# A hybrid RWKV-7 / gated DeltaNet block: block inversions split in two, scores in natural layout, keys normed through token scalars

## The chip, the cores and the metric

The kernel runs on one core of one Trainium2 chip. The metric is the device time of one execution in microseconds (us); a time is the median of several runs. The engines of the core are TensorE (PE, matrix products into PSUM; its weight loads are counted apart as PEld), VectorE (DVE), ScalarE (ACT), GpSimd (POOL) and SyncE (SP, which here only issues transfers). Each engine runs its own instructions in order and waits for the others by semaphores.

## The reference

One layer over 256 latent tokens of width 2048 and a prefix of 256 context tokens. Both are normed and modulated, go through one input projection and through two token mixers, each in both directions: RWKV-7 with 16 heads of 64, and gated DeltaNet with 8 heads of 128. The mixers are merged through sigmoid gates; a SwiGLU feed-forward of hidden width 5632 and a last norm follow. The two recurrences are what the change is about:

```python
def rwkv7_scan(r, w, k, v, kk, bb, s0):
    def step(s, inp):
        r_t, w_t, k_t, v_t, kk_t, b_t = inp
        sa = jnp.einsum('bhij,bhj->bhi', s, kk_t)
        s = s * w_t[:, :, None, :] - sa[..., None] * b_t[:, :, None, :] + v_t[..., None] * k_t[:, :, None, :]
        return s, jnp.einsum('bhij,bhj->bhi', s, r_t)
...
def gdn_chunked(q, k, v, g, beta, s0):     # k and q come in l2-normed
...
    decay = jnp.where(incl, jnp.exp(jnp.where(incl, diff, 0.0)), 0.0)
    kb = kc * bc[..., None]
    lmat = jnp.where(strict, jnp.einsum('nbhik,nbhjk->nbhij', kb, kc) * decay, 0.0)
    rhs = jnp.concatenate([vc * bc[..., None], kb * jnp.exp(gc)[..., None]], axis=-1)
    sol = lax.linalg.triangular_solve(lmat, rhs, left_side=True, lower=True, unit_diagonal=True)
    u, wk = sol[..., :dv], sol[..., dv:]
...
    def step(s, inp):
        qk_i, u_i, w_i, qd_i, kt_i, gl_i = inp
        v_new = u_i - jnp.einsum('bhck,bhkv->bhcv', w_i, s)
        o = jnp.einsum('bhck,bhkv->bhcv', qd_i, s) + jnp.einsum('bhcj,bhjv->bhcv', qk_i, v_new)
        s = s * gl_i[..., None, None] + jnp.einsum('bhck,bhcv->bhkv', kt_i, v_new)
        return s, o
```

## The kernel before

**Stages.** A first stage (to 139 us) computes the modulation and the normed input and splits it into a high and a low fp32r part. The woven stage follows: all other input projections, both mixers and part of the modulation. Then come the merge products (`pa`, `pb`), the output projection, the feed-forward and the last norm, which the change leaves as they are. A full-precision product is made of three fp32r matmuls (weights high by input high, high by low, low by high), so each weight tile passes through a cast on ACT (`whi`) and a subtraction on DVE (`wlo`). These are the `mm` products; all other matmuls of the mixers are plain f32.

**The woven stage** is ordered by a planner, `Weave`, when the program is built. Every piece of work is a Python generator that yields the instructions it wants next, or the name of an event that it needs. A greedy loop keeps a modelled time for each engine and always issues the piece that can start first, with `RANK` to break ties; `LAT` holds the model's delays. The resulting order on PE, DVE, ACT and POOL is fixed in the program. `Words` and `Weave.late` model when PE's instructions arrive, in blocks of 256. The 40 gate products have no early consumer; `GATES_A` and `GATES_B` say after which pair or head each may be taken, and so they fill gaps.

**RWKV pairs.** Two heads of 64 make a pair, in the two halves of the 128 partitions; eight pairs run through `prepare` (decays, keys), `grams` (score matrices by 64-token chunks), `inverse`, `values` and `scan`. In `grams` the scores `X` and the decayed queries `laR` are stored with the heads' halves interleaved, so that masking and scaling take one instruction for each half. `inverse` inverts 16 unit-triangular 64x64 matrices a head through `invert`: the 16x16 diagonal blocks are transposed, sent to a scratch in DRAM (`scr`), read back as one block a partition, solved there by 15 steps of two small DVE instructions, sent back (`tscr`), and combined by small products on PE (`pi` banks) into 32 and 64. Pair p may not begin before the inversion of p - 1 has ended (`yield "inverse", p - 1`).

**DeltaNet heads.** Eight heads run through `features` (convolution, silu, norms by `l2n`), `tokens` (keys and values turned to token layout, keys scaled to `keg` and `kta`), `decays`, `head_grams`, `head_inverse` (the same `invert`, with eight 64x64 matrices, so that the substitution fills 64 partitions, and a last step to 128) and `head_scan`. The last computes `NW`, minus the solved keys, ahead of the recurrence; a step is then PE (solved values plus `NW` by state), DVE (`Vn`), PE (`kta` by `Vn`), DVE (`St`).

All of these go through `Lane.op` (line 148) and, on PE, `Words` (line 198), so they share these two lines in the profile and are told apart by their tiles; `arena` is one large tile in which many others lie, and `inX` another.

Of the kernel before, what the change touches and what calls it, by code (L numbers as in the profile page):

```python
# [11 lines left out]
F32 = mybir.dt.float32  # L12
# [6 lines left out]
P = 128  # L19
D = 2048  # L20
KT = D // P
T = 256
# [5 lines left out]
GATES_A, GATES_B = (6, 3, 2, 3, 0, 1, 4, 3), (3, 2, 0, 1, 1, 1, 9, 1)  # L28

RANK = dict(cast=-98, lowrank=164, prepare=59, grams=34, inverse=-70, values=-6, scan=-95, begin=196, head_scan=145, head_inverse=100, head_grams=132, decays=132, tokens=73, features=120, gate_out=137, lowrank_out=105, row_tile=496)  # L30
LAT = dict(dma=2.04, hop=0.2729, own=0.092, grp=32, cg=4, turn=0.17)
# [7 lines left out]
for _name, _w in (("ident", 128), ("ones", 128), ("bd64", 128), ("rmask", 256),  # L39
                  ("low16", 2), ("eye16", 32), ("tri", 256), ("aft", 256), ("past", 256), ("q4", 4), ("q2", 2),  # L40
                  ("eps", 1), ("gneps", 1)):
    _C[_name] = (_n, _n + _w)
    _n += _w
# [12 lines left out]
def const_array():  # L56
# [20 lines left out]
    put("past", np.where(np.concatenate([u <= v, u >= v], 1), 0.0, -200.0))  # L77
# [25 lines left out]
BLOCK = dict(size=256, first=193, ahead=40, time=4.2, base=8, waits=1.0072)  # L103
# [82 lines left out]
class Words:  # L186


    def __init__(self, engine):
        self.engine, self.n = engine, BLOCK["base"]  # L190

    def __getattr__(self, name):
        if name not in ("matmul", "transpose"):
            return getattr(self.engine, name)

        def op(out, a, *r, **k):
            self.n += (2 if name == "transpose" or a.dtype == F32R else 4) * BLOCK["waits"]
            return getattr(self.engine, name)(out, a, *r, **k)  # L198
        return op


class Weave:
# [5 lines left out]
    def __init__(self):  # L208
        self.work, self.free, self.done, self.now, self.kind = [], {}, {}, 0.0, "split"
        self.block, self.here, self.asked = None, 0.0, None  # L210
# [4 lines left out]
    def late(self, ops, start):  # L215

        n, t, b, here, asked, late = self.tensor.engine.n, start, self.block, self.here, self.asked, 0.0
        if b is None:
            b = int(n - BLOCK["first"]) // BLOCK["size"] + 1
        for o in ops:  # L220
            edge = BLOCK["first"] + BLOCK["size"] * b
            if asked is None and n >= edge - BLOCK["ahead"]:
                asked = max(t, here)
            if n >= edge:
                if t < here:
                    late += here - t
                    t = here
                b, here, asked = b + 1, (t if asked is None else asked) + BLOCK["time"], None
            n += self.words(o) * BLOCK["waits"]
            t += o.cost  # L230
        return late, (b, here, asked)
# [48 lines left out]
    def run(self):  # L280
        while self.work:
# [29 lines left out]
            if lane is self.tensor:  # L311
# [4 lines left out]
                self.block, self.here, self.asked = self.late(ops, start)[1]  # L316
# [9 lines left out]
def emit(ctx: ExitStack, tc, A, out, dbg=None):  # L326
    nc = tc.nc
    V, S, G, Q = nc.vector, nc.scalar, nc.gpsimd, nc.sync
    E = Words(nc.tensor)
# [35 lines left out]
    past = c_("past").rearrange("p (d t) -> p d t", d=2)  # L365
# [252 lines left out]
    def invert(pool, Lt, parts, nu, which, full, fill):  # L618
# [3 lines left out]

        h2 = nu // 2
        late = 0.0 if nu == 16 else 1.2
        sl, tl = scr[which], tscr[which]

        T0 = pool.tile([P, nu, 64], F32, tag="iv0", name="T0")
        Tx = pool.tile([P, nu, 64], F32, tag="ivx", name="Tx", bufs=2)  # L630
        us = (slice(0, h2), slice(h2, nu))
        flip = T0[:, us[0]]
        for h in range(2):
            r = slice(64 * h, 64 * h + 64)
            for u0, ap in parts(h, 0):
                yield v.transpose(flip[r, u0:u0 + ap.shape[1], :], ap)
# [1222 lines left out]
```

## Time and profile before

| | us |
|---|---|
| median of 3 runs | 2201.65 (2200.84 to 2202.81) |
| the profiled execution | 2203.45 |
| its span, first to last instruction | 2201.7 |
| first stage | 0 to 139 |
| woven stage | 139 to about 1238, its tail beside the first merge products to about 1300 |
| merge, output projection, feed-forward, last norm | to 2201.7 |

In the profile, a group of instructions is told as line, engine, operation, tiles written and read (out<-in), shape and count; then busy time in us, the mean of one in ns, and the idle time of the engine before them with what ended it. The kind MATMUL on PE appears twice for a plain f32 product. For a tile, the columns are shortest, median and longest duration in ns and the first and last start in us.

### The profile page before, as it was taken

What the parts mean: (1) busy time and instruction counts of PE and PEld (TensorE: products, weight loads), DVE (VectorE), ACT (ScalarE), POOL (GpSimd) and SP (SyncE); (2) the same over time, 40 slices, a digit from 0 to 9 for tenths busy, and PEclk for the clock granted to TensorE, in tenths of its full rate; (3) what the DMA queues carried; (4) which work ended last, traced back from release to release, by engine and by line L of the source; (5) the groups of instructions that cost most, each with busy time, mean ns of one, the idle gap of its engine ahead of it and who ended that gap; (6) DMA issues with size and microseconds to landing.
All of it is one profiled execution on the core that took longest, in us unless ns stands there. A gap on an engine that the chain in (4) does not pass through costs nothing.

```text
span 2201.7 us, 56730 instructions
## 1 busy us (share of the span) xinstructions
PE 2107.9 (96%) x23996; PEld 1906.1 (87%) x23996; DVE 1576.0 (72%) x3197; ACT 1068.0 (49%) x1852; POOL 121.7 (6%) x203
## 2 busy tenths in 40 slices
PE   6999899999999999999999899999999999999998
PEld 4766687878888778888889899999999999999997
DVE  3456788888898768999998789955665665544544
ACT  3249744554456345555545465534444444444443
POOL 0000000110000010111110010100000000000000
PEclk9999999999999999999999999999999999999999
DMA  9966543444444435666657878927777776566665
GB/s 386 413 178 197 153 127 104 120 123 114 120 120 130 115 105 183 194 184 193 185 186 257 292 282 306 347 85 233 236 232 233 236 236 201 189 186 188 191 186 161
DMA packets 234494, 435.29 MB, mean 198 GB/s; under 512 B 115328, under 2 KB 129664, under 8 KB 229888
## 3 DMA queue, kind: packets, MB, share of 16 engines
q1 hardware_dynamic: 206304, 355.11, 51.4%
q0 software_dynamic: 14112, 51.39, 7.0%
q10 hardware_dynamic: 13824, 25.17, 3.5%
q8 instruction: 188, 3.08, 0.6%
q14 instruction: 66, 0.54, 0.1%
HBM read 405.76 MB, written 25.84 MB: 196 GB/s over the span
## 4 chain that ended last, share of the span: by engine, by line
issue 41%; PE 11%; DVE 6%; DMA 3%; ACT 1%; POOL 1%; SPq 0%; POOLq 0%; DVEq 0%; ACTq 0%
PE mm L198 8%; DVE arena L148 2%; DMA aw<-ada_rest 2%; PE s L198 1%; DVE wlo L148 1%; DVE aw L148 1%; PE pa L198 1%; DMA wraw<-pa 1%; DVE inX L148 1%; PE pi L198 0%; DMA arena<-grow 0%; DVE wlo L413 0%; DMA inX<-tscr 0%; DVE LT L148 0%; ACT arena L148 0%
## 5 line engine op out<-in xcount | busy, mean ns | idle before, releaser
L413 DVE TENSOR_TENSOR wlo<-wraw,whi 128x1024 fp32r<-128x1024 f32 x328 | 392.4, 1198 | 320.6 <-ACT whi L412 318.4
L412 ACT CAST whi<-wraw 128x1024 fp32r<-128x1024 f32 x328 | 337.2, 1029 | 467.3 <-PE mm L198 417.5
L198 PE MATMUL mm<-hxh,wlo 128*128 128x256 f32 (+1 forms) x1408 | 474.8, 337 | 10.0 <-DVE wlo L148 9.3
L198 PE MATMUL mm<-hxh,whi 128*128 128x256 f32 (+1 forms) x1408 | 476.0, 338 | 5.7 <-ACT whi L148 3.2
L198 PE MATMUL mm<-hxl,whi 128*128 128x256 f32 (+1 forms) x1408 | 472.0, 335 | 0.0
L198 PE MATMUL mm<-hfh,wlo 128*128 128x256 f32 x1344 | 375.5, 279 | 0.4 <-DVE wlo L413 0.4
L198 PE MATMUL mm<-hfh,whi 128*128 128x256 f32 x1344 | 375.2, 279 | 0.0
L198 PE MATMUL mm<-hfl,whi 128*128 128x256 f32 x1344 | 375.2, 279 | 0.0
L198 PEld LDWEIGHTS mm<-hxh,wlo 128*128 128x128 f32 x1408 | 267.3, 190 | 39.1 <-DVE wlo L148 14.3
L198 PEld LDWEIGHTS mm<-hxh,whi 128*128 128x128 f32 x1408 | 267.4, 190 | 32.3 <-issue 6.8
L198 PEld LDWEIGHTS mm<-hxl,whi 128*128 128x128 f32 x1408 | 267.6, 190 | 24.6 <-issue 4.4
L148 ACT CAST whi<-wraw 128x512 fp32r<-128x512 f32 x344 | 204.6, 616 | 123.3 <-PE mm L198 82.3
L148 DVE TENSOR_TENSOR wlo<-wraw,whi 128x512 fp32r<-128x512 f32 x344 | 241.8, 704 | 27.8 <-ACT whi L148 24.9
L198 PEld LDWEIGHTS mm<-hfh,wlo 128*128 128x128 f32 x1344 | 252.6, 188 | 0.7 <-DVE wlo L413 0.6
L198 PEld LDWEIGHTS mm<-hfl,whi 128*128 128x128 f32 x1344 | 252.6, 188 | 0.0
L198 PEld LDWEIGHTS mm<-hfh,whi 128*128 128x128 f32 x1344 | 252.6, 188 | 0.0
L198 PE MATMUL mm<-za,whi 128*128 128x256 f32 x1024 | 180.2, 279 | 0.0
L198 PEld LDWEIGHTS mm<-za,whi 128*128 128x128 f32 x1024 | 156.1, 188 | 0.1
L148 DVE TENSOR_TENSOR arena<-arena 128x28 f32<-128x28 f32 (+13 forms) x538 | 138.9, 260 | 19.3 <-DMA arena<-scr 8.5
L198 PE MATMUL mm<-za,wlo 128*128 128x256 f32 x512 | 142.9, 279 | 0.0
L148 ACT ACTIVATE arena<-arena 128x512 f32<-128x512 f32 (+3 forms) x132 | 76.3, 592 | 72.1 <-DVE arena L148 49.2
L198 PEld LDWEIGHTS mm<-za,wlo 128*128 128x128 f32 x512 | 96.2, 188 | 0.0
(316 smaller groups left out, 3618.7 us busy)
## 6 DMA issues: line engine op xcount, KB each, us to landing
wraw<-w SPq DMA_DIRECT2D x172, 512.0 KB, 4.0
wraw<-wgu SPq DMA_DIRECT2D x168, 512.0 KB, 4.7
aw<-ada_rest POOLq DMA_DIRECT2D x96, 512.0 KB, 5.5
aw<-ada_first SPq DMA_DIRECT2D x32, 1024.0 KB, 14.1
wraw<-wdn SPq DMA_DIRECT2D x64, 448.0 KB, 3.6
wraw<-wout SPq DMA_DIRECT2D x32, 512.0 KB, 6.3
aw<-ada_gt ACTq DMA_DIRECT2D x64, 256.0 KB, 5.0
wraw<-wdn SPq DMA_DIRECT2D x32, 512.0 KB, 3.6
```

Of the source, the lines that this page charges most:

```text
L148: return Op(self, cost, lambda: getattr(self.engine, name)(out, *a, **k), kind)
L198: return getattr(self.engine, name)(out, a, *r, **k)
L412: S.copy(hi[:, c, :M], raw[:, c, :M])
L413: V.tensor_sub(lo[:, c, :M], raw[:, c, :M], hi[:, c, :M].bitcast(F32))
```

## The change

For the RWKV pairs, `invert` is split. `solve` does the transposes, the scratch transfers and the 16x16 substitution, in buffers of its own; `invert` does the rest. A pair's `solve` waits for the previous pair's `solve` and for the inversion before that; its `invert` still waits for the previous `invert`. Scores keep the natural layout: `X` has its masked scores in one slot for both halves, the queries are `rin`, their second scores `p2m`, and each is masked or scaled by one instruction over 128 partitions. The products that read them are 64x64 with both halves placed by hand, and the readout of `scan` makes two banks that are added. The identity in `KBx` is filled by ACT instead of POOL.

For the heads, `head_solve` makes the substitution for two heads at once on 128 partitions. Keys stay unnormed: `tokens` sums their squares a token on ACT, and the inverse norms go into the token scalars `gam`, which multiply the scores, the solved values and the values. `keg`, `kta` and `NW` are gone; from the second step on the recurrence computes key by state, corrects the values with it on DVE, then solves, scales on ACT (`Vs`, `Vn`) and updates the state. The decays are relu and exp on ACT instead of a subtraction on POOL and a minimum on DVE, with a mask for the first half alone. The score products with the queries move from `head_grams` to a piece of their own, `outputs`. Several buffers are deeper (keys 4, values, `LT` and outputs 3). `RANK`, `LAT['dma']`, `GATES_A`, `GATES_B` are other numbers, and PE's instruction supply is modelled as a rate with a cap instead of blocks.

```diff
-GATES_A, GATES_B = (6, 3, 2, 3, 0, 1, 4, 3), (3, 2, 0, 1, 1, 1, 9, 1)
+GATES_A, GATES_B = (5, 3, 2, 1, 0, 1, 5, 3), (3, 1, 0, 0, 2, 2, 9, 3)
...
-BLOCK = dict(size=256, first=193, ahead=40, time=4.2, base=8, waits=1.0072)
+BLOCK = dict(cap=160, rate=61.0)
...
+    def solve(pool, X, tt, flips, which, late, fill):
...
+        n = len(flips)
+        for i, (flip, part) in enumerate(flips):
+            u0, m = 16 // n * i, 8 // n
+            for h in range(2):
+                r = slice(64 * h, 64 * h + 64)
+                yield v.transpose(flip[r], part(h, 0))
+                w = dq(unit_rows(sl, h, u0, m), flip[r], 2)
+                w = dq(unit_rows(sl, h, u0 + m, m), part(h, 1), 2)
         yield w + late
...
+            yield v.tensor_mul(pr, X[:, j + 1:, j:j + 1].to_broadcast([P, n, m]), TT[:, j:j + 1, :m].to_broadcast([P, n, m]))
+            yield v.tensor_add(TT[:, j + 1:, :m], TT[:, j + 1:, :m], pr)
...
# prepare, grams
-            for j, h in enumerate(half):
-                yield v.tensor_mul(la[h, d, :, j, :], c3(r)[h], inc[h, 0:4, :])
+            yield v.tensor_mul(rin[:, d], c3(r), inc[:, 0:4, :])
...
-        for j in range(2):
-            h = half[1 - j]
-            yield v.tensor_mul(X[h, d, :, 1 - j, :], c3(p2[h]), mask(1 - d, 0, 8)(h))
+        yield v.tensor_mul(X[:, d, :, 0, :], c3(p2), mask(1 - d, 0, 8)(full))
...
+                yield s.copy(KBx[h, :, :, j, :].rearrange("p d c o -> p (d c) o"), ident[h, h].unsqueeze(1).to_broadcast([64, 16, 64]))
...
-        for j in range(2):
-            h = half[1 - j]
-            yield v.tensor_mul(la[h, d, :, j, :], c3(p2[h, 0:T]), mask(d, 64, 4)(h))
+        yield v.tensor_mul(p2m[:, d], c3(p2[:, 0:T]), mask(d, 64, 4)(full))
...
# inverse
         if p:
+            yield "halved", p - 1
+        if p > 1:
+            yield "inverse", p - 2
...
+        yield from solve(rs, end[:, 0:T], end[:, T:], [(Tx[:, 0:8], lambda h, d: LT[64 * h:64 * h + 64, d])], p % 2, 0.0, g)
+        weave.ready("halved", p)
+        if p:
             yield "inverse", p - 1
...
# features, tokens
-        yield from l2n(k, 512)
+        weave.ready("silu", h)
         yield from l2n(q, T, float(P) ** -0.5)
...
+        for b in range(4):
+            yield s.activation(kt[:, b], ps[:, P * b:P * b + P], AF.Square, accum_out=ssq[:, 0, h, b:b + 1])
+        yield s.copy(kt.rearrange("p b c -> p (b c)"), ps)
+        weave.release(pab)
+        yield s.activation(ssq[:, 0, h], ssq[:, 0, h], AF.Ln, bias=eps)
+        yield s.activation(ssq[:, 2, h], ssq[:, 0, h], AF.Exp, scale=-1.0)
+        yield s.activation(ssq[:, 1, h], ssq[:, 0, h], AF.Exp, scale=0.5)
+        for i, t in enumerate((nbtok, btok)):
+            yield v.tensor_mul(gam[:, i, h], t[:, :, h:h + 9:8], ssq[:, 2, h].unsqueeze(2).to_broadcast([P, 4, 2]))
+        weave.ready("norm", h)
+        yield v.tensor_mul(gam[:, 2, h], gam[:, 1, h], eta[:, :, h:h + 9:8])
...
+        for b in range(4):
+            yield s.activation(vt[:, b], ps[:, P * b:P * b + P], AF.Identity, scale=ssq[:, 1, h, b:b + 1])
-        for d in range(2):
-            col = 8 * d + h
-            late, soon = (slice(0, 4 - d), slice(d, 4))
-            yield v.tensor_mul(keg[:, d, late], p4[:, late], egc[:, late, col:col + 1].to_broadcast([P, 4 - d, P]))
-            yield v.tensor_mul(kta[:, d, soon], p4[:, soon], eta[:, soon, col:col + 1].to_broadcast([P, 4 - d, P]))
...
# decays
-            yield g.tensor_sub(ed, row, gct[:, :, col:col + 1].to_broadcast([P, 4, P]))
-            yield v.tensor_tensor(ed, ed, past[:, d].unsqueeze(1).to_broadcast([P, 4, P]), ALU.min)
-            yield s.activation(ed.rearrange("p b c -> p (b c)"), ed.rearrange("p b c -> p (b c)"), AF.Exp)
+            for b in range(4):
+                yield s.activation(ed[:, b], row[:, b], AF.Relu, bias=gct[:, b, col:col + 1], scale=-1.0)
+            yield s.activation(ed.rearrange("p b c -> p (b c)"), ed.rearrange("p b c -> p (b c)"), AF.Exp, scale=-1.0)
+            yield v.tensor_mul(ed[:, 0:2], ed[:, 0:2], tri[:, d].unsqueeze(1).to_broadcast([P, 2, P]))
...
# head_scan
-        NW = gs.tile([P, 2, 3, P], F32, tag="NW", name="NW")
-        for d in range(2):
-            ps = yield psb
-            yield [e.matmul(ps[:, P * i:P * i + P], keg[:, d, b, :], tf[:, 4 * d + b, :], start=True, stop=True)
-                   for i, b in enumerate(gorder[d][1:])]
...
+            if n:
+                ps = yield psb
+                yield [e.matmul(ps[:, P * d:P * d + P], k[:, P * bs[d]:P * bs[d] + P], St[:, d, :], start=True, stop=True) for d in range(2)]
+                r2 = gs.tile([P, 2, P], F32, tag="rt", name="rt")
+                for d in range(2):
+                    yield v.scalar_tensor_tensor(r2[:, d, :], ps[:, P * d:P * d + P], egc[:, bs[d], 8 * d + h:8 * d + h + 1],
+                                                 rt[d], ALU.mult, ALU.add)
...
-            for d in range(2):
-                yield v.tensor_scalar_mul(Vn[:, d, :], ps[:, P * d:P * d + P], btok[:, bs[d], 8 * d + h:8 * d + h + 1])
+            Vs, Vn = (gs.tile([P, 2, P], F32, tag="Vn", name="Vn") if use else None for use in (n < 3, n > 1))
+            for i, t in ((2, Vs), (1, Vn)):
+                for d in range(2 if t is not None else 0):
+                    yield s.activation(t[:, d, :], ps[:, P * d:P * d + P], AF.Identity, scale=gam[:, i, h, bs[d], d:d + 1])
```

More of the change, by code (lines that the diff above doesn't have):

```diff
@@ L215, in late @@
     def late(self, ops, start):
-        n, t, b, here, asked, late = self.tensor.engine.n, start, self.block, self.here, self.asked, 0.0
-        if b is None:
-            b = int(n - BLOCK["first"]) // BLOCK["size"] + 1
+        left, t, late = self.left + (start - self.seen) * BLOCK["rate"], start, 0.0
         for o in ops:
[L221 to L229, printed above, removed]
+            left, w = min(left, BLOCK["cap"]), self.words(o)
+            if left < w:
+                late += (w - left) / BLOCK["rate"]
+                t += (w - left) / BLOCK["rate"]
+                left = w
+            left += o.cost * BLOCK["rate"] - w
             t += o.cost
-        return late, (b, here, asked)
+        return late, left, t
     def add(self, rank, gen, at=None):
@@ L315, in run @@
                 self.kind = ops[-1].kind
-                self.block, self.here, self.asked = self.late(ops, start)[1]
+                _, self.left, self.seen = self.late(ops, start)
             w[5] = rest or None
@@ L994, in inverse @@
             if d < 2:
-                yield quad([e.matmul(ps[j][r, 64 * c:64 * c + 64], X[half[1 - j], d, c, a], KB[half[1 - j], d, c, :],
-                                     start=True, stop=True) for c in range(8) for j in range(2) for a, r in enumerate(half)])
+                yield quad([e.matmul(ps[j][half[1 - j ^ a], 64 * c:64 * c + 64], X[half[1 - j], d, c, a], KB[half[1 - j], d, c, :],
+                                     start=True, stop=True) for c in range(8) for j in range(2) for a in range(2)])
                 for j in range(2):
@@ L1390, in head_grams @@
         yield "decay", h
+        yield "norm", h
+        yield "mats", NPAIR - 1 if h else NPAIR - 2
+        if h > 1:
+            yield "inverse", NPAIR - 1
+        if h > 2:
+            yield "inv", h - 3
+        k, Ed = o["k"], o["Ed"]
+        o["LT"] = LT = gs.tile([P, 8, P], F32, tag="LTh" if h % 3 == 2 else "LTg", name="LT")
+        ps = yield pab
+        yield [e.matmul(ps[:, P * b:P * b + P], k[:, P * b:P * b + P], k[:, P * b:P * b + P], start=True, stop=True) for b in range(4)]
@@ L1565, in merge_rows @@
     def merge_rows():
-        for n in ("gram", "tok", "decay"):
+        for n in ("outs", "tok"):
             yield n, NGH - 1
```

336 lines of the change are left out of this document (172 added, 164 removed).

## The prediction

> **What bounds the kernel now.** I read the page's busy times first, then a table of stretches, then TensorE's waits, then the inversions' first and last starts, then single instructions for prices.
>
> ```profile
> PE 2107.9 (96%) x23996; PEld 1906.1 (87%) x23996; DVE 1576.0 (72%) x3197; ACT 1068.0 (49%) x1852; POOL 121.7 (6%) x203
> 139.00:1238.00 1099.00, 1048.87 (x14550) 880.77 (x14550) 929.49 (x2238) 591.82 (x1218) 99.84 (x161) 0.99 0.53 156
> 200.00:800.00 600.00, 566.49 (x9544) 469.75 (x9543) 494.54 (x1130) 326.04 (x699) 45.38 (x79) 0.98 0.45 123
> 800.00:1238.00 438.00, 424.15 (x4627) 369.41 (x4625) 398.33 (x1040) 219.70 (x438) 53.08 (x80) 0.99 0.63 194
> 1238.00:1300.00 62.00, 56.38 (x486) 54.19 (x487) 39.52 (x67) 36.26 (x55) 4.47 (x8) 0.92 0.82 295
> 1500.00:1600.00 100.00, 100.00 (x857) 99.87 (x856) 59.98 (x91) 42.98 (x54) 0.00 (x0) 1.00 0.73 234
> ```
>
> The columns of a stretch are its length, then busy PE, weight loads, DVE, ACT, POOL, the granted clock, DMA share and GB/s. The change touches only the woven stage, 139 to about 1300 us: RWKV pairs to 800, heads after. The feed-forward stretch (the last row) has PE at 100% and is not edited, so whatever is won before it is won at the end. In the woven stage PE idles 1099 - 1048.9 = 50.1 us, and 62 - 56.4 = 5.6 us in its tail: 55.7 us together. The gates' products fill its gaps. So the stage is as long as PE's work plus that idle time, and the time falls by PE work removed and idle time removed, nothing else. DVE comes next: 91% (398 of 438 us) in the heads.
>
> ```profile
> PE mm L198 <- DVE wlo L148: 9.3, 11, 3.1
> PE pi L198 <- DVE arena L148: 6.5, 8, 1.6
> PE s L198 <- DVE VX L148: 6.5, 11, 2.3
> PE mm L198 <- ACT whi L148: 3.2, 1, 3.2
> PE s L198 <- ACT arena L148: 2.6, 1, 2.6
> ...
> PE s L198 <- DVE Vn L148: 2.4, 5, 1.0
> PE pi L198 <- DMA arena<-tscr: 2.4, 1, 2.4
> ```
>
> These are PE's waits between 139 and 1300 us: total, times, longest. The `pi` rows, 6.5 + 2.4 = 8.9 us, are the inversions. Of the others DVE releases 9.3 + 6.5 + 2.4 = 18.2 us, ACT 5.8.
>
> ```profile
> L148 ACT COPY Pm<-pi x16: 577/580/585, 276.0 to 785.5; 64x512 f32<-64x512 f32 x16
> L148 DVE STREAM_TRANSPOSE inX<-LT x16: 422/432/444, 810.8 to 1197.3; 64x256 f32<-64x256 f32 x16
> L148 ACT COPY TF<-inX x16: 616/619/624, 861.1 to 1246.2; 64x512 f32<-64x512 f32 x16
> ```
>
> Two such instructions belong to each pair or head, so a period is a seventh of the distance: (785.5 - 276.0) / 7 = 73 us for a pair, (1246.2 - 861.1) / 7 = 55 us for a head. A head's inversion runs from its first transpose (810.8) to the copy into TF (861.1): 50 of the 55 us. The next may not start before, so the inversions set the pace, and the gates only hide it from PE.
>
> **The change, part by part. PE work.**
>
> ```profile
> 874.73 0.38 PE L198 MATMUL s<-inX,TF 128*128 128x128 f32 x2
> 874.94 0.39 PE L198 MATMUL s<-St,arena 128*128 128x128 f32 x2
> 875.17 0.39 PE L198 MATMUL s<-inX,TF 128*128 128x128 f32 x2
> ...
> 888.20 1.02 PE L198 MATMUL pa<-arena,C 128*128 128x512 f32 x2
> ...
> 889.29 0.40 PE L198 MATMUL mm<-hxl,whi 128*128 128x512 f32 x1
> 889.53 0.40 PE L198 MATMUL mm<-hxh,wlo 128*128 128x512 f32 x1
> L198 PE MATMUL s<-TF,keg 128*128 128x128 f32 x96 | 13.8, 283 | 0.0
> ```
>
> A plain f32 matmul leaves two records. From start to start a 128x128 one takes (875.17 - 874.73) / 2 = 0.22 us. The 512-wide one of the key norm takes 889.29 - 888.20 less the product slot behind it (889.53 - 889.29 = 0.24), 0.85 us. The change drops the products keg x tf, 96 records or 48 matmuls: 48 x 0.22 = 10.6 us. The keys are no longer normed across partitions, so eight 512-wide ones go: 8 x 0.85 = 6.8 us. NW x St becomes k x St and kta x Vn becomes kt x Vs, one for one; transposes and score products keep their number. **PE loses 17.4 us.** The natural score layout turns the readout's 16 matmuls of a pair into 32 of 64x64:
>
> ```profile
> L198 PE MATMUL s<-laR,VX 128*64 128x64 f32 x256 | 10.2, 226 | 1.2 <-DVE VX L148 1.0
> L198 PE MATMUL pa<-Pm,X 64*64 64x64 f32 x512 | 9.3, 221 | 0.0
> ```
>
> 256 records of the one took 10.2 us, 512 of the other 9.3: no change.
>
> **DVE and ACT work**, which counts only through PE's idle time:
>
> ```profile
> L148 DVE TENSOR_TENSOR X<-pa,C 64x512 f32<-64x512 f32 x32 | 22.0, 688 | 0.8
> L148 DVE TENSOR_TENSOR laR<-pa,C 64x256 f32<-64x256 f32 x32 | 13.5, 422 | 0.8
> L148 DVE TENSOR_TENSOR laR<-arena 64x256 f32<-64x256 f32 x32 | 13.3, 416 | 0.3
> L148 DVE TENSOR_TENSOR keg<-pa,egc x16: 517/615/691, 791.3 to 1171.4; 128x512 f32<-128x512 f32 x8, 128x384 f32<-128x384 f32 x8
> L148 DVE TENSOR_TENSOR kta<-pa,eta x16: 518/614/690, 792.6 to 1172.5; 128x512 f32<-128x512 f32 x8, 128x384 f32<-128x384 f32 x8
> L148 DVE TENSOR_TENSOR arena<-arena 64x63 f32<-64x63 f32 x32 | 6.9, 215 | 0.8
> L148 DVE TENSOR_TENSOR arena<-arena 64x15 f32<-64x15 f32 x32 | 5.3, 165 | 2.3 <-DMA arena<-scr 1.9
> L148 DVE TENSOR_SCALAR Vn<-s,btok 128x128 f32<-128x128 f32 x64 | 20.8, 338 | 4.7 <-PE s L198 4.6
> L148 DVE SCALAR_TENSOR_TENSOR St<-St,egl,s 128x128 f32<-128x128 f32 x32 | 10.4, 335 | 1.2 <-PE s L198 1.2
> L148 DVE SCALAR_TENSOR_TENSOR arena<-arena 128x512 f32<-128x512 f32 x24 | 19.6, 817 | 0.4 <-ACT arena L148 0.4
> L148 ACT COPY arena<-s 128x128 f32<-128x128 f32 x16 | 3.7, 270 | 10.6 <-PE s L198 10.6
> L148 ACT ACTIVATE arena<-arena 128x128 f32<-128x128 f32 x3 | 0.9, 311 | 0.0
> L148 ACT CAST whi<-wraw 128x512 fp32r<-128x512 f32 x344 | 204.6, 616 | 123.3 <-PE mm L198 82.3
> ```
>
> The first three rows are half-height pairs of instructions that become one full-height instruction of the same length: (22.0 + 13.5 + 13.3) / 2 = 24.4 us less. keg and kta go: 32 x 0.615 = 19.7. The substitution is 30 instructions a head at 165 to 215 ns, about 46 us in all; two heads at a time halve it, 23 less. Vn moves to ACT, 20.8. The key norm's last DVE pass, 8 x 0.817 = 6.5. The decay's masking shrinks to half its width, 16 x (0.688 - 0.422) = 4. New on DVE are the three corrections of each recurrence in both directions, 48 x 0.335 = 16.1, and 24 small factors at some 0.2, 5. **DVE loses 78 us.** ACT gains eighty scalings at 0.27 to 0.31 (23), sixty-four Relu passes at 0.311 (20), thirty-two squares (10), the identity fill moved from POOL, 16 of 64x1024 at some 1.0, an estimate from the 512-wide cast (16), 32 scaled copies of v at 0.27 in place of eight 512-wide, a key copy of 8 x 0.62 and small norms (13); it loses NW and three passes of each key norm, 16 x 0.5 + 24 x 0.62 (23). **ACT gains 59 us.** No DMA is added: scratch and substitution transfers of the heads fall from 10 a head to 9.
>
> The Trainium skill speaks against this exchange: "ScalarE: Activation LUTs", section "Rules for kernel authors", sends multiplications and relu to VectorE. The rows above disagree for this size, 270 ns on ACT against 338 on DVE, both from PSUM. By the page's own figure for a pointer operand (280 ns + 0.833 ns an element), an estimate of 387 ns each, the eighty scalings would be 31 us on ACT instead of 23, and the sum would stay.
>
> **PE's idle time** is the unknown term. Ends: all 55.7 us gone, or a chain that waits longer and brings back what the work saved (+17). Nearest rows: DVE's load over 139 to 1238 falls from 929/1099 = 0.85 to about 851/1071 = 0.79. If a wait grows as load/(1 - load), the 18.2 us behind DVE shrink by a third, 6 us; ACT's load rises from 0.54 to 0.61 and its 5.8 us grow by 2. The inversions stop setting the pace: a pair's substitution starts before the previous inversion ends, and half of the heads' go away. What is late next is PE itself, and the recurrences behind it. I credit this with 9 us, the `pi` rows whole. **Idle time: -6 + 2 - 9 = -13**, a quarter of the way to its lower end. The reorder of priorities and the new model of PE's instruction supply move work about, not its amount; I cost them at nothing, their cover being the gates' products, 40 before and after, and their price inside the two ends.
>
> Sum: -17.4 - 13 = -30.4 us against the profiled execution's 2203.45 (span 2201.7 and 1.75 around it), 2173. The median of the runs, 2201.65, lies 1.8 below that execution: **2171 us**.
>
> **Rivals.** *A, the forecast*: 2160 to 2184, chance 0.52.
>
> *B, the inversions were the true limit*: with the pace gone, most of the idle time goes (45 of 55.7) and the clock of 0.92 in the tail and 0.98 in the pairs rises, some 0.01 of 1161 us, 12 us: 2201.65 - 17.4 - 45 - 12 = about 2127, and up to 2155 if half of it comes true. For it: 50 of 55 us. Against: PE is 95% busy with the fillers, so shorter chains have little left to uncover. The Trainium skill's "Perfetto Trace Analysis", section "Identifying the Most-Contended Engine", judges TensorE by weight loads, not by matmul busy time; by that rule the woven stage (881 of 1099) is 80% used against 100% in the last stretch, which speaks for B. Chance 0.22.
>
> *C, the longer recurrence*: each step but the first now has PE, DVE, PE, ACT where it had PE, DVE.
>
> ```profile
> 1268.11 0.61 DVE L148 TENSOR_SCALAR Vn<-s,btok 128x128 f32<-128x128 f32 x2 [0.50 <-PE s L198]
> ...
> 1273.22 0.61 DVE L148 TENSOR_SCALAR Vn<-s,btok 128x128 f32<-128x128 f32 x2 [1.72 <-PE s L198]
> ```
>
> A step of two links took 5.1 us in the tail, so three more links cost up to 7.7 us a head. Inside a period of 55 us that is free; for the last two heads it can stand bare, 15 us, once the merge products beside them run out: 2201.65 - 17.4 - 8 + 15 = about 2191. Chance 0.16, a quarter of it within 0.2%.
>
> *D, slower: ACT's queue*. It runs in order, and the split products need its casts (the `whi` row: 344). A scaling that waits at its head for a recurrence product holds back the cast behind it, and PE then waits on `whi` or `wlo` for 9.3 / 11 = 0.85 us. From 21 of the 80 scalings on, that eats the 17.4 us; at 35 of them the time is 2201.65 - 17.4 + 30 = about 2214. For it: casts are PE's largest wait already. Against: ACT is half idle. Chance 0.10, a tenth of it within 0.2%.
>
> **How the numbers follow.** 0.2% of this time (4.4 us) is what a measurement can tell from no change. Faster: A, B and three quarters of C, 0.86. Same: 0.05. Slower: 0.09. The range runs from the middle of B to the far end of C, 2140 to 2194, which leaves D and 0.09 of B outside.
>
> **What would show it.** Right: s<-TF,keg gone, the norm's 512-wide records halved, DVE near 1500 us and ACT near 1127 on the page, the feed-forward stretch unchanged but earlier, idle time in the woven stage near 43 us. B shows as under 20 us of it; C as waits of `s` products on ACT or DVE after the last gate; D as more and longer waits of `mm` on `whi` and `wlo`. If PE's work falls and the idle time grows by as much, the step on idle time was wrong.

## The result and the profile after

The changed kernel takes 2184.12 us, the median of 7 runs (2178.58 to 2195.28), against 2202.25 (2198.50 to 2208.21) for the kernel before in the same measurement: a ratio of 0.992 with a 95% interval of 0.989 to 0.994. Measured a second time it took 2183.87 us, with a ratio of 0.992 (0.990 to 0.994). The forecast was 2171. So the kernel is faster, by about 18 us where some 30 were forecast.

The page of the changed kernel (span, then busy time, share and instructions of each engine):

```profile
span 2182.2 us, 56965 instructions
...
PE 2100.9 (96%) x24140; PEld 1906.5 (87%) x24140; DVE 1484.8 (68%) x2974; ACT 1121.0 (51%) x2111; POOL 78.1 (4%) x171
```

DVE came out 15 us under the forecast's 1500, ACT 6 us under its 1127. To see where the time went, cut both traces at the same marks: the last product of the woven stage that reads the normed input (`hxh`), then the first and last starts of the stages behind it. Two stretches of the kernel before, columns as in the prediction (length, then busy PE, weight loads, DVE, ACT, POOL, granted clock, DMA share, GB/s), cut at its last hxh product at 1236.7 us:

```profile
139.00:1236.70 1097.70, 1048.46 (x14549) 880.58 (x14549) 928.20 (x2235) 590.97 (x1215) 98.88 (x160) 0.99 0.53 155
1236.70:1300.00 63.30, 56.79 (x499) 54.37 (x488) 40.81 (x70) 37.12 (x56) 5.43 (x10) 0.92 0.82 295
```

The same of the changed kernel, cut at its last hxh product at 1212.6 us, and the 30 us around that point:

```profile
139.00:1212.60 1073.60, 1040.39 (x14836) 879.85 (x14836) 844.96 (x2042) 651.15 (x1487) 57.58 (x132) 0.99 0.55 162
1212.60:1300.00 87.40, 75.87 (x575) 73.83 (x574) 61.32 (x80) 44.33 (x59) 7.94 (x14) 0.90 0.89 317
...
1215.00:1245.00 30.00, 21.61 (x129) 20.02 (x128) 14.00 (x19) 11.31 (x16) 2.93 (x5) 0.75 0.99 360
```

Up to the last hxh product PE idles 1097.7 - 1048.5 = 49.2 us before and 1073.6 - 1040.4 = 33.2 after. The balance over the whole span, from the first and last starts of the stages' products in the two traces:

| stretch | before, us | after, us | difference |
|---|---|---|---|
| 139 us to the last hxh product | 1097.7 | 1073.6 | -24.1 (PE busy -8.1, idle -16.0) |
| to the last product of the two merge stages | 114.7 | 110.6 | -4.1 (PE busy -8.7, idle +4.6) |
| output projection | 97.2 | 98.3 | +1.1 |
| feed-forward, gate and up | 494.5 | 497.3 | +2.8 |
| feed-forward, down | 246.8 | 251.6 | +4.8 |
| last norm | 11.8 | 11.8 | 0 |
| sum | | | -19.5 |

Up to the last merge product the kernel gained 28.2 us, near the forecast's 30.4. 8.7 us of it were lost again in the stages behind, which the change does not touch. A second pair of traces, of the same two kernels run again, gives 25.0 and 5.4 us for these two sums, so a sum from one pair is good to some 3 us. PE's waits of the changed kernel between 139 and 1300 us (total, times, longest) show the second place to look at:

```profile
PE mm L399 <- ACT whi L389: 5.9, 3, 2.8
PE mm L147 <- DVE wlo L147: 5.4, 8, 2.1
PE pa L147 <- issue: 5.1, 4, 1.9
PE s L147 <- ACT lo L147: 4.1, 7, 1.1
PE pi L147 <- issue: 2.7, 5, 0.9
PE pi L147 <- DMA inX<-tscr: 2.5, 2, 1.9
PE s L147 <- DVE VX L147: 2.5, 7, 0.8
```

The largest is new: L399 is a product of the merge stage, which waits for a weight tile. The waits for `wlo`, `VX` and `Vn` by DVE, 18.2 us before, are 5.4 + 2.5. The inversions' periods fell as they were meant to; copies of a pair's and a head's inversion, with first and last start:

```profile
L147 ACT COPY Pm<-pi x16: 578/582/588, 265.7 to 736.5; 64x512 f32<-64x512 f32 x16
...
L147 ACT COPY TF<-inX x16: 602/617/621, 861.0 to 1161.0; 64x512 f32<-64x512 f32 x16
```

A pair takes (736.5 - 265.7) / 7 = 67 us where it took 73, a head (1161.0 - 861.0) / 7 = 43 where it took 55. The recurrences therefore end at 1192 us in place of 1280, ahead of the last hxh product and no longer behind it.

### The profile page after: what moved, and what is told of

Its sections match the earlier page's. It is cut to its first block, busy times and chain, and to the rows that moved or that the text cites. A ratio compares the mean times of both kernels' runs of the same rounds, so it can differ in the third digit from the quotient of the medians.

```text
span 2182.2 us, 56965 instructions
## 1 busy us (share of the span) xinstructions
PE 2100.9 (96%) x24140; PEld 1906.5 (87%) x24140; DVE 1484.8 (68%) x2974; ACT 1121.0 (51%) x2111; POOL 78.1 (4%) x171
## 4 chain that ended last, share of the span: by engine, by line
issue 54%; PE 24%; DMA 9%; DVE 7%; ACT 4%; POOL 1%; SPq 0%; POOLq 0%; ACTq 0%; DVEq 0%
PE mm L147 14%; PE pa L147 4%; DMA aw<-ada_rest 3%; PE s L147 2%; DVE arena L147 2%; DMA aw<-ada_first 2%; PE pi L147 2%; DVE wlo L147 1%; DMA wraw<-pa 1%; DVE aw L147 1%; DMA wraw<-w_low 1%; ACT arena L147 1%; ACT whi L147 1%; PE mm L494 1%; ACT lo L147 1%
## 5 line engine op out<-in xcount | busy, mean ns | idle before, releaser
L147 PE MATMUL mm<-hxh,wlo 128*128 128x256 f32 (+1 forms) x1376 | 462.5, 336 | 6.0 <-DVE wlo L147 5.6
L147 PE MATMUL mm<-hxh,whi 128*128 128x256 f32 (+1 forms) x1376 | 462.5, 336 | 1.7 <-DVE arena L147 1.7
L147 PE MATMUL mm<-hxl,whi 128*128 128x256 f32 (+1 forms) x1376 | 462.7, 336 | 0.0
L399 PE MATMUL mm<-hfh,whi 128*128 128x256 f32 x1344 | 376.2, 280 | 0.0
L147 PEld LDWEIGHTS mm<-hxh,wlo 128*128 128x128 f32 x1376 | 262.5, 191 | 34.2 <-DVE wlo L147 10.8
L147 DVE TENSOR_TENSOR wlo<-wraw,whi 128x512 fp32r<-128x512 f32 x344 | 235.0, 686 | 78.9 <-ACT whi L147 76.6
L147 PEld LDWEIGHTS mm<-hxh,whi 128*128 128x128 f32 x1376 | 262.8, 191 | 25.2 <-issue 3.1
L147 PEld LDWEIGHTS mm<-hxl,whi 128*128 128x128 f32 x1376 | 262.8, 191 | 24.3 <-issue 4.2
L399 PEld LDWEIGHTS mm<-hfh,whi 128*128 128x128 f32 x1344 | 252.7, 188 | 0.0
L399 PE MATMUL mm<-za,whi 128*128 128x256 f32 x512 | 144.7, 283 | 0.0
L400 PE MATMUL mm<-za,whi 128*128 128x256 f32 x512 | 144.6, 282 | 0.0
L400 PEld LDWEIGHTS mm<-za,whi 128*128 128x128 f32 x512 | 97.6, 191 | 0.0
L399 PEld LDWEIGHTS mm<-za,whi 128*128 128x128 f32 x512 | 97.6, 191 | 0.0
## 6 DMA issues: line engine op xcount, KB each, us to landing
aw<-ada_first SPq DMA_DIRECT2D x32, 1024.0 KB, 13.7
```

Source lines behind the costliest of these rows:

```text
L147: return Op(self, cost, lambda: getattr(self.engine, name)(out, *a, **k), kind)
L399: E.matmul(ps, hi, Xh[:, k, :n], start=first and i == 0, stop=False)
L400: E.matmul(ps, hi, Xl[:, k, :n], start=False, stop=False)
```

## The experiments

All times are set against the kernel before on the same chip. The repeated runs of both kernels come first:

> The changed kernel once more, as the yardstick. In its first trace the edited part (to the last merge product) was 28 us shorter, but the feed-forward products ran slower from some 275 us after their start: 117.8, then 118.9 ns a slot instead of 116.7, which took back 7.6 us. Theory 1 (the slots are a state of the chip in that execution, not of the kernel): here they are 116.7 ns again, the edited part is 28 us shorter, and the time 22 to 28 us below before. Theory 2 (the kernel causes it, by its place in memory or its load on the chip): the same slowing again, and the time 18 to 20 us below before.

> The kernel before, for a second trace of it on the same chip. Theory 1: its feed-forward slots are as likely to be slow as those of the changed kernel on this chip. Theory 2: 116.7 ns throughout, as in its first trace, while the changed kernel's are slow.

Measured: 2183.87 us, ratio 0.992 (0.990 to 0.994), last merge product at 1322.9 us and span 2180.4, so the changed kernel's stage marks repeat within 2 us; and 2201.79 us in the one run of the kernel before, span 2200.0, its last merge product at 1347.9 us where it was at 1351.4. The down projection takes 251.7 us again in the changed kernel and 246.7 in the kernel before: that slowing comes with the kernel, as theory 2 has it. Gate and up take 496.1 and 496.4 us, so the 2.8 us of the table did not come again.

### Is PE's work what the stage is made of?

```diff
# head_scan: 48 products by TF that nothing reads
+        for d in range(2):
+            ps = yield psb
+            yield [e.matmul(ps[:, P * i:P * i + P], kt[:, b, :], tf[:, 4 * d + b, :], start=True, stop=True)
+                   for i, b in enumerate(gorder[d][1:])]
+            weave.release(psb)
...
# features: a 512-wide product for each head that nothing reads
+        ps = yield pab
+        yield e.matmul(ps, ones, k, start=True, stop=True)
+        weave.release(pab)
```

> The changed kernel with the removed TensorE work put back as dead products: six 128x128 f32 products at the start of each head's recurrence and one 512-wide f32 product after each head's silu, their results read by nobody. It is 48 x 0.22 + 8 x 0.85 = 17.4 us of PE work. Theory 1 (the woven stage is PE work plus idle time): 15 to 20 us longer than the changed kernel. Rival (PE has room in that stage, and the gain came from shorter chains and lighter DVE): under 8 us longer.

Measured: 2202.15 us, ratio 1.000 (0.998 to 1.001), 18.3 us over the changed kernel. The woven stage up to its last hxh product, at 1229.3 us:

```profile
139.00:1229.30 1090.30, 1060.24 (x14948) 896.06 (x14947) 846.70 (x2040) 652.19 (x1486) 57.55 (x132) 0.99 0.54 159
```

The stage grew from 1073.6 to 1090.3 us, by 16.7 us, for 19.9 us more of busy PE; its idle time went from 33.2 to 30.1 us. So in the changed kernel PE's work counts nearly one for one, and the rival (under 8 us) falls. The two ratios leave some 5 us either way on the 18.3, and the forecast's 17.4 us lie inside.

### The handover to the merge stage

The SP queue of the changed kernel around the last hxh product (start, duration, transfer, count):

```profile
1208.56 4.05 SPq L386 DMA_DIRECT2D wraw<-pa  x3
1212.76 1.48 SPq L1673 DMA_DIRECT2D gts<-gts__1356  x3
1214.28 1.10 SPq L1083 DMA_DIRECT2D gts__1356<-arena  x1
1215.43 7.69 SPq L1673 DMA_DIRECT2D gts<-gts__1356  x3
1223.22 1.32 SPq L386 DMA_DIRECT2D wraw<-pa  x1
1224.64 0.38 SPq L1689 DMA_DIRECT2D arena<-xT  x1
1225.11 21.03 SPq L386 DMA_DIRECT2D wraw<-pa  x5
```

The merge stage reads the gates back (`gts`) and the input (`xT`) over the same queue that brings its weights (`wraw<-pa`). Between 1212.76 and 1223.22 no weight is issued. The kernel before has such a pause too:

```profile
1229.29 5.80 SPq L409 DMA_DIRECT2D wraw<-pa  x3
...
1237.92 9.51 SPq L1635 DMA_DIRECT2D gts<-gts__1356  x5
1247.53 1.65 SPq L409 DMA_DIRECT2D wraw<-pa  x1
```

But there 144 matmul records of the mixers, 12.9 us, still lie behind the last hxh product, and none of PE's waits from it to the last merge product is for `whi`. In the changed kernel none of that work is left there. The edit moves the half of the gates that is needed later (two of its transfers from POOL's queue to this one), and `xT`, behind weights that are needed first:

```diff
-    for i in range(0, 32, 4):
-        (G if i >= 24 else Q).dma_start(gts[:, i:i + 4], ...)
+    for i in range(0, 16, 4):
+        Q.dma_start(gts[:, i:i + 4], ...)
...
# first merge loop, over j
+        if j in (3, 5, 7, 9):
+            i = 10 + 2 * j
+            tc.keep_in_program_order(Q.dma_start(gts[:, i:i + 4], ...))
...
# second merge loop; the load ahead of the loops goes
+        if j == 5:
+            tc.keep_in_program_order(Q.dma_start(x1, A["xT"]))
```

> The changed kernel with less traffic at the handover from the woven stage to the merge: the second half of the gates is reloaded during the first merge products instead of ahead of them, and the 2 MB of the residual input during the second. In the changed kernel PE is idle 8 of the 30 us from 1215 to 1245, at a granted clock of 0.75, with DMA at 0.99. Theory (the recurrences now end 20 us before the handover, so nothing covers this reload): 6 to 12 us shorter than the changed kernel, PE idle under 4 us in these 30 us. Rival (the weights' own turn through three buffers is the limit there): within 3 us of the changed kernel.

Measured: 2176.87 us, ratio 0.988 (0.986 to 0.990), 7.0 us under the changed kernel. The same 30 us, and PE's waits from 1212 to 1330 us, where the row of 5.9 us for `whi` is gone:

```profile
1215.00:1245.00 30.00, 25.95 (x196) 24.85 (x195) 20.89 (x26) 16.79 (x23) 2.66 (x5) 0.94 0.98 350
```

```profile
PE mm L401 <- DVE wlo L390: 3.7, 3, 2.1
PE mm L400 <- DVE oal L405: 1.9, 2, 1.3
PE mm L399 <- ACT oah L404: 1.8, 1, 1.8
```

Idle time there fell from 8.4 to 4.1 us, just over the 4 expected, and the granted clock rose from 0.75 to 0.94. The last merge product comes at 1318.4 instead of 1323.2 us although the woven stage ended later in this execution (1216.2 against 1212.6). So the order of these loads costs the changed kernel some 7 us, and the rival (within 3 us) falls. How much of that the change itself brought is not shown, since the kernel before was not run with the same edit.

### The slower slots of products that nobody edited

Single products of the down projection, the kernel before and then the changed kernel (start, length, tiles, count):

```profile
2006.37 0.28 PE L198 MATMUL mm<-za,wlo 128*128 128x256 f32 x1
2006.49 0.40 PE L198 MATMUL mm<-za,whi 128*128 128x256 f32 x2
2006.72 0.28 PE L198 MATMUL mm<-za,wlo 128*128 128x256 f32 x1
2006.84 0.40 PE L198 MATMUL mm<-za,whi 128*128 128x256 f32 x2
2007.07 0.28 PE L198 MATMUL mm<-za,wlo 128*128 128x256 f32 x1
```

```profile
1983.26 0.28 PE L401 MATMUL mm<-za,wlo 128*128 128x256 f32 x1
1983.38 0.28 PE L399 MATMUL mm<-za,whi 128*128 128x256 f32 x1
1983.50 0.28 PE L400 MATMUL mm<-za,whi 128*128 128x256 f32 x1
1983.62 0.28 PE L401 MATMUL mm<-za,wlo 128*128 128x256 f32 x1
```

Read from one `wlo` product to the next, three products take 0.35 us before and 0.36 after. PE is never idle in either and the clock is whole, so neither row of busy time shows it. Averaged over the trace, a product with `za` takes 116.7 ns before and 120.0 in the repeated run of the changed kernel, one with `zb` 116.7 in both. The change dropped 256 constant columns and added 288 for `ssq` and `gam`, which moved the weight buffers up by 128 bytes in each partition; `za` stayed, and `zb` moved down by 896, since the arena is 256 columns shorter. The first edit restores all three places in the changed kernel; the second moves `za` alone in the kernel before.

```diff
# in the changed kernel
-    arena = arp.tile([P, 9288], F32, name="arena")
+    arena = arp.tile([P, 9544], F32, name="arena")
...
-    ssq = cst.tile([P, 3, NGH, 4], F32, name="ssq")
+    ssq = cst.tile([P, 2, NGH, 4], F32, name="ssq")
+    rsq = arena[:, 9512:9544].rearrange("p (h b) -> p h b", h=NGH)
...
# in the kernel before
     W4 = zap.tile([P, 2, 4, KT, P], F32R, tag="za", name="w4")
+    zap.tile([P, 32], F32, name="gap")
```

> The changed kernel with its buffers put back where the kernel before has them: 32 of the new columns (the keys' norms) go into the arena, which gets its 9544 columns back. Nothing that is computed and no instruction changes. Two theories for the half-hour-glass of the slots: in the kernel before, a product of the down projection takes 116.7 ns with either half of its input (za, zb); in the changed kernel 120.0 ns with za and 116.7 with zb, and the products of the first stage (hxh, hxl) 118.1 against 117.1. Theory 'place': the slot hangs on the number of bytes between the moving operand and the weights, which the change shifted by 128 for za and hxh and by 1024 for zb. Then za's products take 116.7 ns again and hxh's about 117.1: 1536 x 3.3 ns = 5.1 us and some 2290 x 1.0 ns = 2.3 us, so 7 us off the changed kernel, ratio about 0.988 to 0.990. Rival 'history': the slot is settled by how the stage is entered, and stays at 120 ns: ratio 0.991 to 0.993 as the changed kernel.

> The kernel before with one unused tile of 128 bytes per partition in the pool of za, which moves za (and the weights w4 that lie there earlier) down by 128 bytes and nothing else; no instruction changes. Theory 'place': za's products take 120 ns in place of 116.7, zb's stay: 1536 x 3.3 ns = 5.1 us more, ratio about 1.002. Rival 'history': 116.7 ns and ratio 1.000 within its interval.

190 us of the down projection, all busy with PE at clock 1.00, one row each for the kernel before, the changed kernel, the restored places, and the kernel before with `za` moved; the count behind PE's busy time tells the slot:

```profile
1960.00:2150.00 190.00, 190.00 (x1631) 190.00 (x1631) 94.25 (x99) 82.85 (x99) 0.00 (x0) 1.00 0.65 188
```

```profile
1960.00:2150.00 190.00, 190.00 (x1598) 190.00 (x1597) 91.91 (x97) 81.09 (x97) 0.00 (x0) 1.00 0.64 184
```

```profile
1960.00:2150.00 190.00, 190.00 (x1631) 190.00 (x1630) 94.52 (x101) 83.15 (x100) 0.00 (x0) 1.00 0.66 189
```

```profile
1960.00:2150.00 190.00, 190.00 (x1607) 190.00 (x1605) 92.68 (x97) 81.23 (x97) 0.00 (x0) 1.00 0.64 186
```

The kernel before with `za` moved took 2205.51 us, ratio 1.003 (1.002 to 1.004): one unused tile of 128 bytes makes it slower. Its down projection took 250.4 us; in that trace gate and up took 499.1 us as well, a stage whose length also moves between executions of one kernel. The restored places gave 2178.51 us, ratio 0.991 (0.989 to 0.994). Its down projection is back at 246.7 us, and hxh's products of 256 columns are at 117.1 ns from 118.1, which is some 2 us of the woven stage (an estimate from about 2200 such products); but its six runs spread from 2174 to 2193 us, and the time as a whole does not separate from the changed kernel's 0.992. So the place sets the slots, and the 5 us of the stage are read from its trace. The theory's rule, the distance between operand and weights, did not hold as stated: with `za` moved in the kernel before, `za` products took 118.6 ns and `zb` products 117.8, where 120 and 116.7 were expected, and `zb`'s own distance had not changed. The runs with products put back and with the values on VectorE show that pattern too, at the very addresses of the changed kernel. Which of the two slow patterns comes is open.

### Both amends together

> Both amends together: the buffers where the kernel before has them, and the later half of the reload of the gates spread over the first merge stage with the load of xT in the second. If the two costs are separate, the 7.0 us that the spread reload gave and the 7 us of the place add up: about 2170 us, ratio 0.985; by the rival (place does nothing) 2177 us, ratio 0.988, as the spread reload alone.

Measured: 2174.53 us, ratio 0.988 (0.987 to 0.990), against an expected 0.985. It is faster than both kernels, but not shown to be faster than the spread reload alone (0.988); the time is the one that the rival gives. The profiled execution has a span of 2168.4 us: last merge product at 1312.8, down projection 246.7, so the place does show in the trace.

### The halves of the inversions

```diff
# inverse, pairs
         if p:
-            yield "halved", p - 1
-        if p > 1:
-            yield "inverse", p - 2
+            yield "inverse", p - 1
...
-        if p:
-            yield "inverse", p - 1
...
# head_solve
-            yield "solved", i - 1
+            yield "inv", 2 * i - 1
...
-        if i > 1:
-            yield "inv", 2 * i - 3
```

Both edits at once, the pairs' alone, and the heads' alone:

> The changed kernel with the halves in series again: a pair's solve waits for the whole inversion of the pair before, and a head's solve for both inversions of the head before, as one did before the change; all instructions stay. Theory 'overlap buys waits' (the prediction's: nine microseconds of waits for the inversion): the recurrences end later (last product with TF from 1192 towards 1280 us), idle time of PE in the woven stage goes up by 4 to 10 us, and in return the handover after it is covered again (idle at 1215 to 1245 us from 8 down to 3 us): net 0 to 6 us slower than the changed kernel, ratio 0.992 to 0.995. Rival 'overlap buys nothing': the waits stay as they are in the changed kernel and only the handover is better covered: some 4 us faster, ratio 0.990.

> Only the pairs in series: a pair's solve waits for the whole inversion of the pair before; the heads keep the two at a time. With both in series the kernel took 1.0101 of the time before, with the overlap 0.992; PE's idle time up to the last hxh product was 54.7 against 33.2 us. Theory 'two chains': the overlaps pay one by one, each in its own part of the woven stage (with both in series the first product with TF came 18 us later, the last hxh product 27 us later, so about two thirds lie with the pairs): ratio 0.999 to 1.005, idle time 44 to 50 us. Rival 'ranks': what costs is that the ranks and due times were made for the overlapped order and any wait upsets them: then half of it undone costs nearly as much as both, ratio over 1.006.

> Only the heads in series: a head's solve waits for both inversions of the head before; the pairs keep their halves. Theory 'two chains': the third of the loss that came after the first product with TF, 8 to 15 us more than the changed kernel: ratio 0.995 to 0.999, idle time up to the last hxh product 37 to 43 us, the recurrences' end later than 1192 us. Rival 'ranks': as above, ratio over 1.002. Second rival 'slack': the heads' chain has slack now that it ends 20 us before the last hxh product, and nothing is lost: ratio 0.990 to 0.993.

| | us | ratio (95%) | over the changed kernel's 0.9919 | idle to the last hxh product, us |
|---|---|---|---|---|
| both | 2220.58 | 1.010 (1.008 to 1.012) | 0.0182, 40 us | 54.7 |
| pairs | 2206.12 | 1.003 (1.001 to 1.004) | 0.0107, 24 us | 48.1 |
| heads | 2199.12 | 0.999 (0.997 to 1.001) | 0.0073, 16 us | 43.1 |

With both in series the kernel is slower than the kernel before, although it lacks the products of 17.4 us. Its woven stage and its waits from 139 to 1300 us:

```profile
139.00:1239.40 1100.40, 1045.74 (x14807) 878.95 (x14808) 840.86 (x2032) 649.46 (x1483) 55.96 (x130) 0.99 0.53 156
```

```profile
PE mm L147 <- DVE wlo L147: 10.5, 18, 1.3
PE mm L399 <- ACT whi L389: 8.5, 1, 8.5
PE s L147 <- DVE VX L147: 5.1, 13, 1.1
PE pi L147 <- issue: 5.0, 7, 1.4
```

The stage is as long as before (1100.4 against 1097.7 us). So the expectation for both missed by far: neither 0 to 6 us slower nor 4 faster, but 40 slower. The pairs' and the heads' shares, 24 and 16 us, add up to the 40. That speaks for two chains, each paying in its own part, and against the rival by which any half undone costs nearly all. The heads' share and idle time lie just beyond the expected bounds, and the second rival, slack in the heads, falls. These three orders also hold 4, 4 and 3 more table loads on ACT, 1.28 us each, so the wait that was put back and the new order are not parted. Up to the last hxh product PE's idle time is 21.5 us longer with both in series than in the changed kernel. Little of this comes back under the inversions' name: the `pi` rows have 9.7 us against 7.9, `wlo` 10.5 against 5.4, `VX` 5.1 against 2.5, and the rest is spread over many rows. My reading, which no run shows, is that PE takes the filling products early once the chain sets the pace, and then waits for their weights.

### Which engine scales, and in which order

```diff
# head_scan
-                    yield s.activation(t[:, d, :], ps[:, P * d:P * d + P], AF.Identity, scale=gam[:, i, h, bs[d], d:d + 1])
+                    yield v.tensor_scalar_mul(t[:, d, :], ps[:, P * d:P * d + P], gam[:, i, h, bs[d], d:d + 1])
```

> The 80 scalings Vn back from ScalarE (367 ns each) to VectorE; nothing else. The prediction gave relief of VectorE 6 us and the load on ScalarE minus 2, for all the instructions that change engine. Theory 'small': VectorE gains some 25 to 30 us of work and ScalarE loses 29, and PE waits 0 to 4 us more: ratio 0.991 to 0.994. Rival 'ScalarE behind': ScalarE's queue holds back the casts of the weights (PE's longest waits in the woven stage name whi by ScalarE), and without the Vn PE waits 3 to 6 us less: ratio under 0.990.

Measured: 2192.66 us, ratio 0.996 (0.994 to 0.998), some 10 us over the changed kernel; both theories missed, the rival in its sign. A scaling took 343 ns on DVE in this run, 367 on ACT in the changed kernel:

```profile
L147 DVE TENSOR_SCALAR Vn<-s,gam x80: 300/343/352, 871.0 to 1208.9; 128x128 f32<-128x128 f32 x80
```

```profile
L147 ACT ACTIVATE Vn<-s,gam x80: 352/367/419, 868.5 to 1192.9; 128x128 f32<-128x128 f32 x80
```

Those are the instructions of tile Vn in this run and in the changed kernel (shortest, median, longest). PE's largest wait of this run is elsewhere:

```profile
PE mm L399 <- ACT whi L389: 14.6, 1, 14.6
PE mm L147 <- DVE wlo L147: 7.2, 14, 1.8
```

One wait of 14.6 us for a merge weight, where the changed kernel has 5.9 in three. In the changed kernel one weight is issued between the reload of the gates and the load of `xT` (1223.22 and 1224.64); here `xT` is issued first (1230.06) and the next weight only at 1231.52. Up to the last hxh product this run is 7.5 us longer, 4 of them idle, and through the merge stages another 4. What moving the scalings costs by itself is therefore not parted from the order that came with it.

Last, the planner's account of PE's instruction supply, put back to that of the kernel before. PE's, DVE's and POOL's instructions are the same and only their order differs; ACT has four more table loads.

```diff
-BLOCK = dict(cap=160, rate=61.0)
+BLOCK = dict(size=256, first=193, ahead=40, time=4.2, base=8, waits=1.0072)
# and Words and Weave.late of the kernel before
```

> The planner's account of PE's instruction supply as it was in the kernel before (blocks of 256 words); the instructions are the same, only their order by the planner may differ. The prediction costed the new account at nothing: ratio 0.990 to 0.994. Rival 'order': the account was a part of the gain, and the order by the old one costs 5 us or more: ratio over 0.9945.

Measured: 2198.02 us, ratio 0.9985 (0.997 to 1.000), 14.5 us over the changed kernel; the rival holds. Its woven stage to the last hxh product has 44.8 us of idle time against 33.2, with as many matmul records (14836):

```profile
139.00:1225.20 1086.20, 1041.35 (x14836) 879.83 (x14836) 841.82 (x2040) 656.47 (x1490) 55.97 (x132) 0.99 0.54 160
```

## Why the prediction was right, and where not

The median of 2184 us lies at the upper edge of A (2160 to 2184), not far from C's 2191. The time alone does not tell these two apart; the traces do.

**The work of PE, -17.4 us: right**, by the run that put it back (18.3 us). That the natural layout costs nothing on PE is borne out: the 512 records with `rin` and `p2m` take 9.8 us together, the 256 with `laR` took 10.2. The sum up to the last merge product is a weaker witness: PE's busy time fell by 8.1 + 8.7 = 16.8 us in the first pair of traces and by 11.7 in the second. That sum also holds the slower slots of hxh's products, which work against it.

**The idle time, -13 us: right in size, wrong in make-up.** It fell by 16.0 - 4.6 = 11.4 us in the first pair and by 13.2 in the second. The prediction's list of waits left rows out: all `pi` rows together had 13.7 us and not 8.9. They did not go, but fell to 7.9, by 5.8 us where 8.9 were credited. The rows behind DVE, credited with 6, lost 18.2 - 7.9 = 10.3. That the sum came out is partly luck, since these two errors go opposite ways. The price of the overlap was misread more deeply. I gave it 9 us, the waits that name the inversions; in series the changed kernel loses 40 us, and its woven stage is as long as that of the kernel before. A chain that sets the pace need not show its price under its own name. Rival B, the inversions as the true limit, fits the kernel with its halves in series. It falls for the changed kernel, whose idle time is 33.2 + 11.5 = 44.7 us to the last merge product (43 forecast; under 20 by B). The Trainium skill's "Perfetto Trace Analysis", section "Identifying the Most-Contended Engine", which goes by weight loads and the share of peak, has weight loads in 880 of 1074 us of the woven stage, 82%, after the change; the run with the products back shows that it is nearly full for PE's work nonetheless.

**The planner costed at nothing: wrong.** Of the same matmuls one order takes 14.5 us more than another. The kernel before had numbers made for its own work, so this does not say that the change gained 14.5 us by its order. It says that every experiment here that alters the order carries such a term. The losses of the series runs and of the values on VectorE contain an unknown part of it, though the products put back also changed the order and showed no idle time for it. No run gave an undone part an order of its own; that stays open.

**"Whatever is won before it is won at the end": this step failed**, and with it most of the 12.3 us between the forecast's 30.4 and the medians' 18.1. In the first pair of traces 8.7 us of it were lost behind the merge stages, 0.6 + 1.6 us are missing in the two terms above, and 1.4 us lie between the spans, which are 19.5 us apart, and the medians. Of the 8.7 us, the 4.8 of the down projection came again in the second pair (5.0) and go away when the buffers are put back. The 2.8 in gate and up did not come again: the stage takes 497.3 and 496.1 us in the two profiles of the changed kernel, 494.5 and 496.4 in those of the kernel before, and up to 499.1 in the others. What moves it is not explained.

**The handover: a term that the prediction did not have.** I counted the recurrences' early end as a gain only. Behind the last hxh product PE idles 11.5 us where it idled 6.9, and spreading the reload gave 7.0 us back; no rival named it. That the recurrences used to cover the reload fits the two kernels, but it is not shown as the cause. The runs with both or the heads in series have 28 such records (4.7 us) behind their last hxh product, and they idle more there, 14.5 and 13.0 us.

**C and D fell.** The longer recurrence (C) has no bare tail, since the recurrences end 20 us before the last hxh product. Held-back casts (D) would have raised the waits on `wlo` in the woven stage; these fell from 9.3 to 5.4 us, and the run without the scalings on ACT was slower, though its order changed as well. A scaling's record is longer than the forecast had it: 367 ns, not 270 to 311. The Trainium skill's "ScalarE: Activation LUTs", section "What ACT_TABLE_LOAD costs", has 280 ns + 0.833 ns an element with one pointer operand, an estimate of 387 for 128 columns, which is nearer. The sum on ACT was near all the same (+53 us, +59 forecast), because consecutive ACT instructions overlap. The decays took the 64 Relu passes of the forecast, 32 on `Ed` and 32 on `inrin`, each near 400 ns where the forecast had 311; but four of them are done in 1.27 us:

```profile
719.42 1.27 ACT L147 ACTIVATE Ed<-arena,gct 128x128 f32<-128x128 f32 x4
L147 ACT ACTIVATE Ed<-arena,gct x32: 386/402/433, 719.4 to 993.5; 128x128 f32<-128x128 f32 x32
L147 ACT ACTIVATE inrin<-arena,gct x32: 386/394/418, 759.2 to 1034.1; 128x128 f32<-128x128 f32 x32
```

The 80 scalings keep ACT busy for 25.7 us in all (23 forecast), the Relu passes for 22.2 (20). The durations of all ACT instructions together grew by 84 us.

## What to carry to other kernels

A wait's name tells which instruction came last, not which chain sets the pace: before pricing a chain by its rows, compare its period with the stage. In the same way, a sum of durations is not busy time on an engine whose instructions overlap. When a change lets a stage's producers end earlier, ask what their work was covering at the next stage's entry, above all loads that share a queue with that stage's weights. And after adding or dropping a buffer, compare the slot of one unedited product in both traces: a shift of 128 bytes was worth 4 to 5 us here, and no row of busy or idle time showed it.

## What the hardware showed beyond that

The slot of a 128x256 fp32r product depended on where its operands lie: 116.7 ns at the places of the kernel before, 118.6 to 120 with an operand that was moved against its weights by 128 bytes in each partition, with PE never idle and the clock at 1.00. `zb`, whose distance to the weights changed by 896 + 128 = 1024 bytes, stayed at 116.7 in the repeated run, but went to 117.8 when `za` alone was moved. The Trainium skill's "SBUF — State Buffer", section "SBUF: two separate sides", says that PE never waits for another on that memory. No run here looked for another engine as the cause; they do show a dependence on place, whose mechanism is open.

The sum of squares on ACT leaves a second instruction for each pass, 32 of them (ACTIVATION_READ_ACCUMULATOR) at 206 ns, which the forecast did not count. They begin before the pass has ended, at 751.8 after 751.6 us for the first, so the 64 instructions together keep ACT busy for 10.5 us, and the forecast's 10 stands.

```profile
L147 ACT ACTIVATE kt<-pa x32: 268/278/302, 751.6 to 1049.0; 128x128 f32<-128x128 f32 x32
L147 ACT ACTIVATION_READ_ACCUMULATOR kt<-pa x32: 192/206/227, 751.8 to 1049.2; 128x1 f32 x32
```
